# Layer 0's MLP in two stages over both halves, with seven-product groups, and a denser selection in blocks 2 to 7

## Chip, core and metric

The kernel runs on one core of a Trainium2 chip. The metric is device time of one execution in microseconds (us), from the start of the program to its end; several executions are timed and the median is given. A profile of one further execution shows each engine: PE (TensorE, the matrix engine; PEld is its weight load), DVE (VectorE), ACT (ScalarE), POOL (GpSimd) and SP (SyncE, which here only issues DMAs). Each engine works through its own instructions in program order and waits on semaphores for the others.

## What is computed

Two decoder layers on a sequence of 1024 tokens of width 1024, in float32. Layer 0 mixes tokens by attention over selected keys (mixer A), layer 1 by a sliding window (mixer B); both read a fixed memory and end in a gated MLP with a causal convolution of width 3.

```python
for i in range(DEPTH):                                  # DEPTH = 2
    h = rmsnorm(x, g_mix[i])
    mix, q_mem = mixer_a(h, ...) if i == 0 else mixer_b(h, ...)
    mem_o = memory_cross_attention(q_mem, mem_n, w_mem_kv[i])
    x = x + jnp.concatenate([mix, mem_o], axis=-1) @ w_out
    x = x + conv_glu_ffn(rmsnorm(x, g_ffn[i]), f_w_up[i], f_conv_w[i], f_conv_b[i], f_w_down[i])
return rmsnorm(x, g_final)

# in mixer_a, for each block of 128 queries (8 blocks): only the 256 best-scored keys are read
score = jnp.where(causal[None], score, -jnp.inf)
_, idx = lax.top_k(score, 256)

def conv_glu_ffn(h, w_up, conv_w, conv_b, w_down):      # D_FF = 2816
    a, b = jnp.split(h @ w_up, 2, axis=-1)
    a = sum(conv_w[j] * a_pad[:, j:j + S] for j in range(3)) + conv_b
    return (jax.nn.silu(a) * b) @ w_down
```

## The kernel before, in words

**Tiles.** Activations lie feature-major: a tile `t` holds 128 features by 2 x 512 tokens. Tokens come in two halves of 512, features of the MLP in NF = 22 tiles of 128 (tile f has a column of `a` and a column of `b`). Every float32 product is made of three matmuls (`mm3`, L256 to L258) of a rounded high part and a low rest; a weight of 128 x 1024 is loaded by SP, its high part made by ACT (L99) and its rest by POOL in two pieces (`rest`, L279). `Weights` loads five ahead and splits `SPLIT` = 2 ahead. All SBUF work tiles share 51 slots. PSUM has four tiles `pB` (128 x 512) and two tiles `pS` (128 x 1024).

**Order.** Nothing is scheduled by a planner: the Python code emits the instructions in their order. Work that is to lie beside the matmuls is a generator; `tick(ns)` moves a clock along with the matmuls emitted and advances each generator by the time it yields. So a yield's size says how densely a background work is spread, and `finish_bg` emits what is left of one at once. Stores go to SP 4 us of that clock later than they are asked for.

**Selection.** `topk` (L1230 to L1321) finds for a set of blocks the 256th best score by 32 rounds of a bit search: in each, DVE counts for one part of the blocks (L1254), ACT for the other (`sign`, L1274), and DVE makes the next candidates (L1265, L1267, twice). Then come passes on DVE alone that settle ties and make masks (L1286 to L1321). Blocks 2 and 3 run beside the query projections (`a_q`), with a yield of 1400 per step; the rest of it is emitted by `finish_bg` ahead of the third unit of attention of half 0. Blocks 4 to 7 run beside half 0's attention (`run_a`) and beside half 0's MLP, with a yield of 2400.

**Layer 0.** Half 0: `run_a`, output projection (`every`), the MLP (`ffn`). Then the same for half 1. `ffn` works on input with the gain but without the norm's scale (`prepare`, `gained`), so that matmuls can start before the norm is known; the scale multiplies `a` (L801, DVE) and the gated value (L811, POOL). For each tile: 24 matmuls for `a`, 24 for `b`; convolution on DVE (L803, L804), Silu on ACT (L810), the product with `b` on DVE (L816). After each second tile the down projection of an earlier pair (48 matmuls into `pS`) is added to x by DVE (L867). The gated values stay in SBUF. All weights are loaded and split once per half.

**Layer 1.** `ffn_up` works on normed input of both halves at once: three tiles in the plain way for each half, then 19 tiles by `group`, which makes the four products of two input halves by two token halves from seven products of half size (84 matmuls for both halves of a tile where the plain way takes 96). The factors on the input's side are made by `right_factors`, those of the weights by `Weights._factor`. Gated values go to DRAM (`keep`, `G_d`), and `ffn_down` reads them back (`fetch`) for both halves with one load of each weight.

## Time and profile before

| | us |
|---|---|
| median of 3 runs | 2623.87 (2623.51 to 2623.92) |
| the profiled execution | 2622.18 |
| its span, first to last instruction | 2620.4 |
| PE busy | 2457.7 (94%), 11912 instructions |
| DVE busy | 1702.1 (65%) |
| POOL busy | 1389.7 (53%) |
| ACT busy | 1205.3 (46%) |

In the profile, "busy" is the time in which an engine has an instruction in work, and a wait is given with the engine, tile and line that ended it. The trace gives these stretches: the query projections run from 209.5 to 359.1, half 0's attention and output projection from 378.6 to 530.6, half 0's MLP with what follows it to 945.9, half 1's attention and output projection to 1113.4, half 1's MLP to 1507.5, layer 1's MLP from 1904.1 to 2603.0.

### The profile page before, as it was taken

To read this page: it belongs to the slowest core of one execution; us is meant where nothing else is said; L and a number is where in the kernel's file an instruction comes from. 1 tells how busy PE (TensorE), PEld (TensorE's weight loads), DVE (VectorE), ACT (ScalarE), POOL (GpSimd) and SP (SyncE) were. 2 spreads that over 40 slices of the span, in tenths; PEclk is the share of its full clock that TensorE was granted. 3 is DMA by queue.
4 is the path that set the end of the run, shared out by engine and by line. 5 is a ranking of instruction groups with operands and counts; after the bars stand their busy time and mean duration, and the time that the engine had idled before them with its cause. 6 is when DMAs were issued, how large, how long until landed. Compare 5 with 4: busy or idle time off the path is not lost. (4 is left out here: it accounts for less than half of the span.)

```text
span 2620.4 us, 34001 instructions
## 1 busy us (share of the span) xinstructions
PE 2457.7 (94%) x11912; PEld 2057.2 (79%) x11912; DVE 1702.1 (65%) x2961; ACT 1205.3 (46%) x2268; POOL 1389.7 (53%) x1241
## 2 busy tenths in 40 slices
PE   7789977999998999999999989999989999999997
PEld 5677866877886888877888878878767888888886
DVE  7887878867777466655553353498786556564446
ACT  5355665645543555433333334588644444442003
POOL 5644133456666633365766665566656666664204
PEclk8899998999999999999999999999989999999999
DMA  5453353422223343332333345642253232348401
GB/s 202 149 168 116 119 173 127 157 79 98 97 74 99 133 161 101 113 101 82 107 122 97 99 117 187 216 139 86 81 193 137 105 121 97 124 170 330 141 15 65
DMA packets 121083, 333.83 MB, mean 127 GB/s; under 512 B 13008, under 2 KB 29904, under 8 KB 120912
## 3 DMA queue, kind: packets, MB, share of 16 engines
q1 hardware_dynamic: 120912, 331.66, 37.7%
q8 instruction: 94, 1.54, 0.2%
q14 instruction: 77, 0.63, 0.1%
HBM read 258.21 MB, written 73.40 MB: 127 GB/s over the span
## 5 line engine op out<-in xcount | busy, mean ns | idle before, releaser
L279 POOL TENSOR_TENSOR t<-t,t 128x512 fp32r<-128x512 f32 x829 | 1109.4, 1369 | 686.6 <-ACT t L99 283.3
L256 PE MATMUL pB<-t,t 128*128 128x512 f32 (+3 forms) x1824 | 682.5, 374 | 9.0 <-DVE t L781 4.1
L258 PE MATMUL pB<-t,t 128*128 128x512 f32 (+3 forms) x1824 | 679.0, 372 | 5.4 <-POOL t L279 5.4
L257 PE MATMUL pB<-t,t 128*128 128x512 f32 (+3 forms) x1824 | 679.6, 373 | 4.5 <-DVE t L461 2.4
L256 PE MATMUL pS<-t,t 128*128 128x512 f32 (+1 forms) x1460 | 573.3, 393 | 45.8 <-DVE t L867 19.4
L257 PE MATMUL pS<-t,t 128*128 128x512 f32 (+1 forms) x1460 | 567.9, 389 | 2.6 <-DVE t L512 2.6
L258 PE MATMUL pS<-t,t 128*128 128x512 f32 (+1 forms) x1460 | 567.1, 388 | 2.7 <-POOL t L279 2.4
L256 PEld LDWEIGHTS pB<-t,t 128*128 128x128 f32 (+1 forms) x1824 | 347.0, 190 | 69.1 <-DVE t L781 4.7
L258 PEld LDWEIGHTS pB<-t,t 128*128 128x128 f32 (+1 forms) x1824 | 346.6, 190 | 66.9 <-POOL t L279 6.7
L257 PEld LDWEIGHTS pB<-t,t 128*128 128x128 f32 (+1 forms) x1824 | 346.8, 190 | 64.2 <-DVE t L461 3.3
L256 PEld LDWEIGHTS pS<-t,t 128*128 128x128 f32 x1460 | 281.3, 193 | 104.6 <-ACT t L99 21.0
L99 ACT CAST t<-t 128x1024 fp32r<-128x1024 f32 x284 | 288.2, 1043 | 101.3 <-PE pS L258 44.1
L258 PEld LDWEIGHTS pS<-t,t 128*128 128x128 f32 x1460 | 280.8, 192 | 62.0 <-POOL t L279 6.3
L257 PEld LDWEIGHTS pS<-t,t 128*128 128x128 f32 x1460 | 281.6, 193 | 53.8 <-DVE t L512 3.0
L265 DVE TENSOR_TENSOR t<-pB,t 128x512 fp32r<-128x512 f32 (+3 forms) x248 | 149.8, 623 | 87.2 <-ACT t L264 84.6
L264 ACT CAST t<-pB 128x512 fp32r<-128x512 f32 (+3 forms) x248 | 126.2, 535 | 160.2 <-PE pB L258 99.7
L1055 DVE TENSOR_TENSOR t<-t,pS 128x1024 f32<-128x1024 f32 (+1 forms) x92 | 107.9, 1174 | 125.6 <-PE pS L258 125.4
L867 DVE TENSOR_TENSOR t<-t,pS 128x1024 f32<-128x1024 f32 x88 | 106.9, 1217 | 54.8 <-PE pS L258 54.5
L811 POOL TENSOR_TENSOR t<-t,t 128x512 f32<-128x512 f32 x44 | 58.4, 1328 | 155.0 <-ACT t L810 155.0
L1447 POOL TENSOR_SCALAR t<-t,st 128x128 f32<-128x128 f32 (+3 forms) x64 | 47.8, 749 | 138.3 <-DVE st L1446 77.8
L1274 ACT ACTIVATE sign<-t,ti 128x1024 bf16<-128x1024 f32 (+1 forms) x96 | 96.5, 1006 | 52.5 <-DVE ti L1267 39.6
L1222 DVE SCALAR_TENSOR_TENSOR t<-t,wtok,t 128x384 f32<-128x384 f32 (+5 forms) x90 | 98.8, 1098 | 22.6 <-ACT t L1217 18.7
(228 smaller groups left out, 3018.9 us busy)
## 6 DMA issues: line engine op xcount, KB each, us to landing
t<-in_up SPq DMA_DIRECT2D x138, 512.0 KB
t<-in_down SPq DMA_DIRECT2D x66, 512.0 KB
G_d<-t SPq DMA_DIRECT2D x44, 512.0 KB
t<-G_d SPq DMA_DIRECT2D x44, 512.0 KB
t<-in_a_in SPq DMA_DIRECT2D x34, 512.0 KB
t<-in_b_in SPq DMA_DIRECT2D x28, 512.0 KB
t<-in_a_out SPq DMA_DIRECT2D x20, 512.0 KB
t<-x_d SPq DMA_DIRECT2D x20, 512.0 KB
```

The source lines that it names most:

```text
L99: nc.scalar.copy(hi[:, :w], raw[:, :w])
L256: mm(out, a[0], b[0], start=start, stop=False, skip_group_check=again)
L257: mm(out, a[0], b[1], start=False, stop=False, skip_group_check=again)
L258: mm(out, a[1], b[0], start=False, stop=stop, skip_group_check=again)
L264: nc.scalar.copy(hi, src)
L265: nc.vector.tensor_tensor(lo, src, hi.bitcast(F32), op=OP.subtract)
L279: self.nc.gpsimd.tensor_tensor(lo[:, s], src[:, s], hi[:, s].bitcast(F32), op=OP.subtract)
L811: nc.gpsimd.tensor_tensor(v, v, rb[0], op=OP.mult)
L867: nc.vector.tensor_tensor(x[dp][:, :, t], x[dp][:, :, t], S, op=OP.add)
L1055: nc.vector.tensor_tensor(xp, xp, S, op=OP.add)
L1222: nc.vector.scalar_tensor_tensor(work[:, :n], tmp[:, :n], wv, work[:, :n], op0=OP.mult, op1=OP.add)
L1274: nc.scalar.activation(hits("sign")[:, :wide], self.work[blks[i]][:, :wide], AF.Sign, bias=cand[:, i:i + 1].bitcast(F32), accum_out=cnt[:, ...
```

## The change

- Layer 0's MLP is made as layer 1's: an up stage that writes the gated values to DRAM, then `ffn_down` for both halves. The up stage of half 0 takes its first four tiles on unscaled input and goes on with normed input until the selection and the first two units of half 1's attention are emitted; the program that results has 17 tiles there. Half 1 takes the same 17 tiles in the same way, and the last five tiles go through `ffn_groups` (formerly the second part of `ffn_up`).
- `right_factors` for layer 0 also rebuilds half 0's split input from DRAM (`h0`). The scale is applied once (`finish`), and the mult on POOL (L811) stays for the first four tiles alone.
- Weights are split four ahead in these stages. `conv` reads `a` from PSUM where the input is normed.
- Selection: blocks 2 and 3 with a yield of 1000 instead of 1400; blocks 4 to 7 with 1200 instead of 2400 from the MLP on.
- The memory units of half 1 begin after the selection, so most of their second parts now lie in half 1's attention. The keys and values of layer 1's memory and the norm of half 0 lie in `ffn_down`.

```diff
-    def ffn(self, l, halves, fold=1, last=None, then=None):
...
+    def ffn_half(self, l, fs, hf, h, rb=None, ahead=None):
+        nc, name = self.nc, f"up{l}"
+        for f in fs:
+            a, b = self.psB(), self.psB()
+            wa = self.w.get(name, f)
+            first = rb is not None and not rb
...
+            self.proj(a, wa, h)
...
+            if rb:
+                nc.vector.tensor_tensor(v, a, rb[0], op=OP.mult)
+            self.conv(l, f, hf, v if rb else a, u)
+            if not first:
+                wb = self.w.get(name, NF + f)
...
+                self.proj(b, wb, h)
+            nc.scalar.activation(u, u, AF.Silu)
+            if rb:
+                nc.gpsimd.tensor_tensor(u, u, rb[0], op=OP.mult)
+            nc.vector.tensor_tensor(u, u, b, op=OP.mult)
+            self.keep(f, hf, u)
...
-            bt.append(self.add_bg(self.topk((2, 3), 1400, (3,))))
+            bt.append(self.add_bg(self.topk((2, 3), [1000], (3,))))
...
-            late.append(self.add_bg(self.topk((4, 5, 6, 7), 2400, (6, 7))))
+            late.append(self.add_bg(self.topk((4, 5, 6, 7), late_pace, (6, 7))))
...
+        def finish(x, sqs, rb, gain, h, wait, keep, dst):
+            yield from self.scale_of(sqs, rb, wait)
+            del sqs[:]
+            yield from self.norm_apply(rb[0], x, gain, 2, h, 2500, keep=keep)
+            yield from self.store_x(x, dst)
...
+        last = self.run_a(0, att, x, mem_o, bm, hook)
+        late[1] = 0.0
+        self.every(last)
...
+        late[1], late_pace[0] = 1.0, 1200
...
+        self.w.SPLIT = self.AHEAD
+        self.ffn_half(0, range(4), 0, raw, rb)
+        del raw[:]
+        while len(h0) < 4:
+            self.tick(100)
+        n_half = 4
+        while bt in self.bg:
+            self.ffn_half(0, [n_half], 0, h0)
+            n_half += 1
...
+        last = self.run_a(1, att, x, mem_o, bm, hook)
+        self.every(last)
...
+        bT = self.add_bg(self.right_factors(hf1, h1, B, h0))
+        self.w.SPLIT = self.AHEAD
+        self.ffn_half(0, range(4), 1, raw, rb)
...
+        self.ffn_half(0, range(4, n_half), 1, h1, ahead=self.AHEAD)
+        self.finish_bg(bn, bT)
...
+        self.ffn_groups(0, b11, b21, b22, B, range(n_half, NF), self.near_down(xs))
...
+        bk = self.add_bg(mem_kv(), 0.4)
...
+        self.ffn_down(0, xs, [hook0, hook1], 3)
+        self.finish_bg(bk)
```

How the order moves is seen at three places. `t` are work tiles, `ti`, `tc` and `hit` the selection's candidates, counts and marks.

DVE, at the end of the query projections, from the memory queries' evacuation (L620, L622) on; first before, then now (the count, L1254, is L1213 there):

```order
L715 TENSOR_REDUCE st<-pB 128x2
L620 SCALAR_TENSOR_TENSOR t_3573<-pS,t_3573 64x1024
L622 SCALAR_TENSOR_TENSOR t_3574<-pS,t_3574 64x1024
L1265 TENSOR_SCALAR ti<-tc 128x1
L1267 SCALAR_TENSOR_TENSOR ti<-ti 128x1
L1254 TENSOR_SCALAR hit,tc<-t_1134,ti 128x384
```

```order
L715 TENSOR_REDUCE st<-pB 128x2
L620 SCALAR_TENSOR_TENSOR t_3638<-pS,t_3638 64x1024
L622 SCALAR_TENSOR_TENSOR t_3639<-pS,t_3639 64x1024
L265 TENSOR_TENSOR t_3658<-pB,t_3658 128x384
L1398 ISA t_3665,st<-pB,t_1134 128x384
```

Before, the rest of the selection of blocks 2 and 3 (45 DVE and 4 ACT operations in the source) stands between L622 and the next evacuation of a `pB` (L265); now none of it does, and it all stands earlier.

DVE, at the start of half 0's MLP, the sum of squares that the norm's matmul (PE, L424) waits for; before, then now:

```order
L412 TENSOR_TENSOR t_5119<-t_5119,t_5143 128x1024
L412 TENSOR_TENSOR t_5119<-t_5119,t_5174 128x1024
L404 TENSOR_TENSOR t_5119<-t_5119 128x512
L404 TENSOR_TENSOR t_5198<-t_5198 128x512
L412 TENSOR_TENSOR t_5119<-t_5119,t_5198 128x512
```

```order
L412 TENSOR_TENSOR t_5119<-t_5119,t_5143 128x1024
L1213 TENSOR_SCALAR hit,tc<-t_1921,ti 128x640
L412 TENSOR_TENSOR t_5119<-t_5119,t_5174 128x1024
L1213 TENSOR_SCALAR hit,tc<-t_2241,ti 128x768
L1224 TENSOR_SCALAR ti<-tc 128x2
L1226 SCALAR_TENSOR_TENSOR ti<-ti 128x2
L404 TENSOR_TENSOR t_5119<-t_5119 128x512
L404 TENSOR_TENSOR t_5198<-t_5198 128x512
L412 TENSOR_TENSOR t_5119<-t_5119,t_5198 128x512
```

Now operations of the selection stand between the sums; before, the selection started again only behind the norm.

ACT, one tile of half 0's MLP in the middle of the bit search, from one convolution's start to the next; before, then now (L1233 is L1274 before, L862 is L802, L908 is L810, L875 is L820):

```order
L802 ACTIVATE t_6234<-t_6234,conv 128x512
L806 COPY prev_a<-t_6234 128x2
L810 ACTIVATE t_6234<-t_6234 128x512
L820 CAST t_6272<-t_6234 128x512
L99 CAST t_6278<-t_6110 128x1024
L1274 ACTIVATE sign,tc<-t_2525,ti 128x1024
L1274 ACTIVATE sign,tc<-t_2846,ti 128x1024
L99 CAST t_6320<-t_6187 128x1024
L802 ACTIVATE t_6325<-t_6325,conv 128x512
```

```order
L862 ACTIVATE t_6041<-pB,conv 128x512
L866 COPY prev_a<-pB 128x2
L99 CAST t_6048<-t_5997 128x1024
L1233 ACTIVATE sign,tc<-t_2567,ti 128x1024
L1233 ACTIVATE sign,tc<-t_2902,ti 128x1024
L908 ACTIVATE t_6041<-t_6041 128x512
L875 CAST t_6091<-t_6041 128x512
L99 CAST t_6098<-t_6046 128x896
L1233 ACTIVATE sign,tc<-t_2567,ti 128x1024
L1233 ACTIVATE sign,tc<-t_2902,ti 128x1024
L862 ACTIVATE t_6142<-pB,conv 128x512
```

A tile now carries two rounds of the search where it carried one.

## Rows read from the trace of the kernel before

**Rows 1.** The page, parts 1 and 2: PE's busy time, its granted clock in slices.

```profile
PE 2457.7 (94%) x11912; PEld 2057.2 (79%) x11912; DVE 1702.1 (65%) x2961; ACT 1205.3 (46%) x2268; POOL 1389.7 (53%) x1241
...
PEclk8899998999999999999999999999989999999999
```

**Rows 2.** Stretches: length, busy us (instructions) of PE, PEld, DVE, ACT, POOL; clock, DMA.

```profile
209.50:359.00 149.50, 144.10 (x673) 119.28 (x672) 120.70 (x231) 97.34 (x209) 36.64 (x31) 0.99 0.31 100
...
432.00:520.00 88.00, 88.00 (x524) 76.67 (x523) 76.18 (x201) 60.46 (x132) 39.10 (x45) 1.00 0.50 168
...
753.50:822.30 68.80, 59.46 (x254) 48.40 (x252) 64.49 (x74) 15.85 (x22) 41.87 (x25) 0.95 0.31 99
...
1904.00:1991.00 87.00, 74.69 (x301) 58.46 (x300) 69.19 (x75) 40.27 (x51) 50.24 (x32) 0.92 0.53 188
1991.00:2353.00 362.00, 362.00 (x1599) 299.75 (x1598) 210.62 (x317) 158.91 (x286) 227.85 (x175) 1.00 0.34 118
```

**Rows 3.** PE and DVE in order of time, 378 to 404: start, us, line, wait.

```profile
378.81 1.47 PE L1434 MATMUL pB<-t,t 128*128 128x384 f32 x6
403.78 0.58 PE L713 MATMUL pB<-t,t 128*128 128x256 f32 x1 [23.50 <-DVE t L265]
...
382.53 1.23 DVE L622 SCALAR_TENSOR_TENSOR t<-pS,t 64x1024 fp32r<-64x1024 f32 x1
...
403.16 0.56 DVE L265 TENSOR_TENSOR t<-pB,t 128x384 fp32r<-128x384 f32 x1
```

**Rows 4.** DVE's waits, 200 to 380: for whom, us in total, times, longest.

```profile
DVE t L1222 <- ACT t L1217: 18.7, 26, 1.4
```

**Rows 5.** PE's waits in half 0's MLP, 530.6 to 946.

```profile
PE pS L256 <- DVE t L867: 14.3, 5, 7.9
PE pS L424 <- DVE t L412: 4.9, 1, 4.9
```

**Rows 6.** PE and DVE in order of time around the first norm of half 0's MLP.

```profile
543.77 1.87 PE L424 MATMUL pS<-ones,t 128*128 128x1 f32 x8 [4.88 <-DVE t L412]
...
542.08 1.63 DVE L412 TENSOR_TENSOR t<-t,t 128x512 f32<-128x512 f32 x1
```

**Rows 7.** DVE by line, 556 to 823: count, busy us, mean ns, idle before.

```profile
L1254 DVE TENSOR_SCALAR_CACHE_REDUCE hit<-t,ti 128x768 bf16<-128x768 f32 x21 | 21.2, 1008 | 0.3
L1267 DVE SCALAR_TENSOR_TENSOR ti<-ti 128x2 int32<-128x2 int32 x42 | 20.3, 482 | 1.4
L1254 DVE TENSOR_SCALAR_CACHE_REDUCE hit<-t,ti 128x640 bf16<-128x640 f32 x21 | 18.3, 873 | 0.0
L1265 DVE TENSOR_SCALAR ti<-tc 128x2 int32<-128x2 f32 x42 | 16.9, 403 | 0.7 <-ACT sign L1274 0.2
```

**Rows 8.** Two such small operations in order of time, DVE, from 739.

```profile
739.81 1.22 DVE L1265 TENSOR_SCALAR ti<-tc 128x2 int32<-128x2 f32 x1
741.06 0.16 DVE L1267 SCALAR_TENSOR_TENSOR ti<-ti 128x2 int32<-128x2 int32 x1
```

**Rows 9.** DVE by line in layer 1's plain tiles, 1935 to 1992.

```profile
L944 DVE SCALAR_TENSOR_TENSOR t<-pB,conv,t 128x511 f32<-128x511 f32 x5 | 3.7, 742 | 3.5 <-ACT t L943 3.5
L971 DVE TENSOR_TENSOR t<-t,pB 128x512 f32<-128x512 f32 x5 | 3.4, 683 | 2.7 <-PE pB L258 1.4 <-ACT t L970 1.3
```

**Rows 10.** PE's waits in half 0's attention, 378.6 to 530.6.

```profile
PE pB L752 <- DVE t L265: 1.6, 4, 0.8
```

**Rows 11.** PE's waits in half 1's MLP, 1113.4 to 1507.5.

```profile
PE pS L256 <- DVE t L867: 5.1, 5, 2.4
PE pS L424 <- DVE t L412: 3.9, 1, 3.9
PE pB L443 <- DVE st L439: 2.8, 1, 2.8
```

**Rows 12.** PE's waits in layer 1's plain tiles, 1904 to 1991, and in its down stage.

```profile
PE pB L258 <- POOL t L279: 5.4, 3, 3.3
...
PE pS L256 <- DVE t L1012: 1.8, 1, 1.8
```

More of the change, by code (lines that the diff above doesn't have):

```diff
@@ new lines, in keep @@
+    def keep(self, f, hf, u):
+        t = self.t4(2, HT, dt=R32)
+        self.nc.scalar.copy(t[:, 0], u)
+        self.rest(t[:, 1], u, t[:, 0])
+        self.store("G", self.G_d[f][hf], t.bitcast(F32))
+    def ffn_half(self, l, fs, hf, h, rb=None, ahead=None):
+        nc, name = self.nc, f"up{l}"
+        for f in fs:
+            a, b = self.psB(), self.psB()
+            wa = self.w.get(name, f)
+            first = rb is not None and not rb
+            if first:
+                split = self.w.SPLIT
+                self.w.SPLIT = max(3, split)
+                wb = self.w.get(name, NF + f)
+            self.proj(a, wa, h)
+            uv = self.t4(2, HT)
+            u, v = uv[:, 0], uv[:, 1]
+            if first:
+                self.proj(b, wb, h)
+                while not rb:
+                    self.tick(100)
+                self.w.SPLIT = split
+            if rb:
[3 more added lines that the diff above has]
+                wb = self.w.get(name, NF + f)
+                if ahead and f == fs[-1]:
+                    self.w.SPLIT = ahead
+                self.proj(b, wb, h)
+            nc.scalar.activation(u, u, AF.Silu)
[3 more added lines that the diff above has]
+            self.keep(f, hf, u)
+            del a, b, uv, u, v, wa, wb
@@ L1015, in group @@
             yield
-            keep(f, 0, ua)
+            self.keep(f, 0, ua)
             tt(ub, ub, c22, op=OP.mult)
             yield
-            keep(f, 1, ub)
+            self.keep(f, 1, ub)
         before = iter(())
-        for f in range(n_std, NF):
+        for f in fs:
             g = group(f)
@@ L1060, in weights @@
             return [self.w.get(f"down{l}", 2 * c + i) for i in range(2)]
-        for c in range(nch - 2):
+        for c in range(nch - tail):
             us = weights(c)
             for hf in range(2):
-                if c + 1 + hf < nch:
-                    fetch(c + 1, hf)
+                self.fetch(c + 1, hf)
                 down(c, us, G.pop((c, hf)), hf)
-        us = [weights(c) for c in (nch - 2, nch - 1)]
-        for hf in range(2):
-            fetch(nch - 1, hf)
-        for hf in range(2):
-            for c, u in zip((nch - 2, nch - 1), us):
-                down(c, u, G.pop((c, hf)), hf)
+        us, cs = {}, range(nch - tail, nch)
+        order = [(c, hf) for hf in range(2) for c in cs]
+        for i, (c, hf) in enumerate(order):
+            if hf == 0:
+                us[c] = weights(c)
+            for e in order[i + 1:i + 3]:
+                if e not in G:
+                    self.fetch(*e)
+            down(c, us[c], G.pop((c, hf)), hf)
     def a_small(self, hf, h):
@@ L1493, in begin_a @@
             yield s()
+        while not selected():
+            yield 500
         for u in units[:2]:
@@ L1720, in run @@
         self.exps = []
-        self.cn, self.work, self.vB, self.qm, self.marks = {}, {}, {}, {}, set()
+        self.cn, self.work, self.vB, self.qm, self.marks, self.G = {}, {}, {}, {}, set(), {}
         self.scratch()
@@ new lines, in run, with memory, begin @@
+        h0, rb = [], []
+        bn = self.add_bg(finish(x, sqs, rb, g[:, 3], h0, 1000, lambda i, t: self.store("hf", self.hf_d[i], t),
+                                self.x_d[0]))
+        del x
+        late[1], late_pace[0] = 1.0, 1200
+        mem = self.mem_units(1)
+        def memory():
+            while late in self.bg:
+                yield 1000
+            self.load_qmem(1)
+            yield 9000
+            yield from self.whole(mem[0], 2200)
+        att = self.attn_a(1)
+        def begin():
+            while ("found", 4) not in self.marks:
+                yield 500
+            yield from self.spread(self.begin_a(att, lambda: late not in self.bg), 2950)
```

357 lines of the change are left out of this document (138 added, 219 removed).

## The prediction

> **What bounds the kernel now.** I read the page first: PE is busy for 94% of the span, at full clock nearly everywhere [rows 1]. So time goes away only where PE gets fewer matmuls, or where one of its waits ends. The stretches come next. In layer 1's groups PE never waits: 1599 matmuls in 362.0 us, 0.2264 us each [rows 2]. That is the pace; a stage's **loss** is its length minus its large matmuls at that pace, minus some 0.15 us for each small one (an estimate, by width). A loss is a wait and the slower clock behind it. Last I read PE's waits by stage, and who ended them.
>
> - Half 0's attention: one wait of 23.5 us. PE stands from 380.3 to 403.78 for a `pB` that DVE empties at 403.16; DVE had been ready at 383.8 (382.53 + 1.23) and then worked through the rest of the selection of blocks 2 and 3 [rows 3].
> - Half 0's MLP (415 us): 1584 large matmuls at the pace are 358.6, some 164 small ones 24, so 33 are lost; the two largest waits are 14.3 for the additions into x, on two `pS`, and 4.9 for the first norm [rows 5].
> - Half 1's MLP (394 us): 358.6, and 116 small ones for 16, so 20 are lost; waits 5.1, 3.9 and 2.8 [rows 11].
>
> **Part 1: five tiles by seven products.** A tile takes 84 matmuls instead of 96 for both halves, 5 x 12 = 60 fewer, 60 x 0.2264 = **-13.6 us**. The groups' additions on DVE and splits on POOL are those of layer 1, where DVE is busy for 58% and POOL for 63% and PE does not wait [rows 2]. Without that cover the five groups (95 us) would lose what layer 1's plain tiles lose (below), 23% or 22 us. The down stage has as many matmuls as before and needs each weight once instead of twice; its transfers through DRAM lie beside it, as in layer 1, where it waits once, 1.8 us [rows 12].
>
> **Part 2: blocks 2 and 3 sooner.** What stands between 383.8 and 403.2 on DVE is emitted earlier, so PE's `pB` comes at about 384.9: 18.9 us are saved, and some 4.6 stay, in which DVE empties the memory queries. The 19 us of DVE work now lie in the query projections, where DVE was busy for 120.7 of 149.5 us [rows 2]: it comes to some 139, 93%. The cover is DVE's own idle time: 18.7 us in 26 holes of 0.7 us, behind ACT [rows 4]. The highest share that a stage without a wait of PE shows is 76.18 of 88.0, 87% [rows 2]. So the added loss lies between 0 and the 9 us by which 139 exceeds 87% of 149.5; I take 4. **-15 us** (bounds -19 and -10).
>
> **Part 3: half 0's up stage.** It has 17 tiles, 816 large matmuls, 185 us, for a selection that had 350. Two losses are to be expected.
>
> *The first norm.* The sum that PE's L424 waits for is ready at 543.7, when PE has waited 4.9 us [rows 6]. Now two counts and three pairs of small operations, or four, stand among the sums: about 0.87 + 1.01 + 0.87 and six times 0.44 [rows 7], 5 us more. The wait is 10 us; with the slow clock behind it, as now, the first tile loses 14 instead of 7.
>
> *VectorE's balance.* A round of the search costs DVE 1.01 + 0.87 + 2 x (0.48 + 0.40) + 0.16 = 3.8 us [rows 7]. From the first tile to the search's end there are 438 matmuls, 99 us, and 18 rounds, 68; nine convolutions and products at 2 x 0.74 + 0.68 [rows 9], 19; the norm's multiplications and rests, 11 (an estimate at 1.0 and 1.2 us); the scaling of `a` in four tiles, 3. That is 101. The passes behind the search were 46 us of DVE: 64.5 busy [rows 2] less eight additions and three tiles' convolution, 18. Now they fall into 47 us of matmuls, with four tiles' work and evacuations, 11: 57. Together 158 us of work in 146. DVE can't be busy all the time, since it waits for ACT's `sign`; in the passes it reached 94%, in the attention 87%. At 92% the 158 take 172, and DVE falls 26 us behind. PE notices only when it needs a `pB` back: there are four, two per tile, so one is needed again three projections (3 x 24 x 0.2264 = 16.3 us) after it is full, less 2.3 for the convolution: 14 us of backlog are free, and weights split four ahead leave about as much. So 12 us are lost here, and after the passes 44 us of matmuls with 17 us of DVE work clear the rest. At 100% the loss is 0, at 85% it is 26. Loss of the stage: 14 + 12 = 26 instead of 33, **-7 us** (bounds -19 and +7). ACT comes close too: four `sign` a tile.
>
> A row speaks against this sum. The small operations of a round take 0.16 us, or 1.22, in the same stretch [rows 8], and in the mean 0.40 and 0.48 [rows 7]. The Trainium skill (SBUF — State Buffer, "Who interferes with whom") says that a DVE instruction with two SBUF inputs, or in a two-port mode, and a GpSimd instruction that reads SBUF exclude each other for the whole instruction. By that, the convolution from PSUM (0.74, with one input in SBUF) should be spared, which the trace agrees with, and a denser search may be blocked more often; the sum above takes the mean as it was.
>
> **Part 4: half 1's attention.** It waits for nothing now. 36 matmuls of the memory units' second parts are left to be emitted at once there, as 48 were in half 0's, where they cost several short waits, four of up to 0.8 us for one cause [rows 10], and slow clock, some 5 us in all. **+4 us** (0 to +8).
>
> **Part 5: half 1's MLP and the down stage.** The additions' waits go with `ffn`'s interleaving [rows 11]; the first norm's stays (7 us with the slow clock). Layer 1's start, with norm and factors beside plain tiles, loses 20 of 87 us, waiting for splits [rows 2, 12]; four splits ahead instead of two should cover all but some 2. The down stage adds its start, 1.8 us, with slow clock 3, and the norms of the memory and of half 0, now on its two `pS`, 8: one such wait is 2.8 [rows 11], twice, with slow clock. 20 against 20: **0 us** (-6 to +8). Layer 1's own code is the same but for names and the order of temporaries; nothing is counted.
>
> **Sum.** -13.6 - 15 - 7 + 4 + 0 = -31.6. The profiled execution took 2622.18, so 2590.6; the median of the runs is 1.7 above it: **2592 us**.
>
> **Rivals.**
>
> *VectorE's backlog is free* (chance 0.17). It keeps at 95% or more; half 0 loses the first norm alone, and the query projections nothing: 2592 - 12 - 4 = 2576. For it: no `pB` of the MLP made PE wait before, however late DVE was. Against: the balance above.
>
> *The selection's denser part gains nothing* (0.12). The query projections turn DVE-bound: the added 19 us reappear as waits for evacuation. 2592 + 15 = 2607. For it: 93%. Against: the holes.
>
> *The splits starve* (0.09). ACT stands behind DVE in both halves, and the splits come late as in layer 1's plain tiles; 23% on half 1's tiles 4 to 12, nine of 10.9 us, is 23 us: 2615.
>
> *VectorE and GpSimd lock each other out; slower* (0.10). If every small operation of the 18 rounds took 1.22 instead of 0.44 us [rows 7, 8], 72 x 0.78 = 56 us come on top of a backlog that is past what is free: 2592 + 56 = 2648. It decides in half 0's MLP, and the kernel is slower than before from 32 us on, when more than half are blocked. For it: POOL's splits are as dense as before while the search is twice as dense. Against: a third were blocked before. The skill's rule above is this rival's; blocked each time is its upper end.
>
> *The change does what it says*: 17 and 5 tiles are in the order, so no chance is set aside for the contrary.
>
> **How the numbers follow.** The forecast has 0.52, the others 0.17, 0.12, 0.09 and 0.10. The forecast's own bounds: all good ends -13.6 - 19 - 19 + 0 - 6 = -58, all bad ones -13.6 - 10 + 7 + 8 + 8 = -1; taken as independent about half of that on either side, 2576 to 2608. The range takes in the first two rivals with their spread and most of the third, 2568 to 2616; outside are the locked case, and the edges, 2 in 10. Within 0.2% (5 us, about what a measurement of this kernel can tell from no change) is 2619 to 2629: 0.06, from the bad ends of the second and third. Slower: 0.11, the lock and a little. Faster: 0.83.
>
> **What would show it.** Right: 60 fewer matmuls; PE's wait for L713 at about 5 us instead of 23.5; a wait for L424 near 10 us; in half 0's tiles waits of PE for a `pB` or a split in the passes behind the search, 5 to 20 us; none for additions into x in half 0's stretch. Wrong: a DVE that is idle in half 0's tiles while PE waits (then it is ACT, POOL or SP that I have costed at nothing); waits on L279 or L99 in half 1's tiles or groups; a loss of over 10 us in the query projections; a clock below full in the down stage. What would make it wrong most easily is the share that DVE can keep up, which no stage of before shows at this density.

## The result, and the profile after

The changed kernel takes 2664.82 us, median of 4 runs (2661.78 to 2666.09); the kernel before took 2623.89. The ratio is 1.0153, with a 95% interval of 1.0138 to 1.0169: **slower** by 41 us, 1.5%. The prediction was 2592, its range ended at 2616. The profiled execution took 2664.9, its span is 2663.1.

The page shows the 60 matmuls gone (11852 where [rows 1] has 11912), PE busy for 13.6 us more all the same, and a lower clock in half 0's MLP and in half 1's.

```profile
PE 2471.3 (93%) x11852; PEld 2060.0 (77%) x11852; DVE 1751.2 (66%) x3005; ACT 1204.9 (45%) x2284; POOL 1295.2 (49%) x1164
...
PEclk9799999989999998999999999999999999999999
```

To say where the time went I took the prediction's loss for every stage: its length minus what its matmuls take at the median distance that their shape keeps in the same trace. The two spans differ by 42.7 us, and this is how they come about (the last column is what the prediction's terms make of the loss before; "rest" is the difference of all other stages together):

| stage | loss before | loss after | difference | predicted loss |
|---|---|---|---|---|
| query projections and the step behind them | 12.0 | 22.1 | +10.1 | 16 |
| half 0's attention | 34.5 | 14.2 | -20.3 | 15.6 |
| half 0's MLP | 33.0 | 47.9 | +14.9 | 26 |
| half 1's attention | 1.8 | 17.1 | +15.3 | 5.8 |
| half 1's MLP and down stage | 19.6 | 45.2 | +25.6 | 20 |
| layer 1's plain tiles | 19.9 | 27.1 | +7.2 | 19.9 |
| rest | | | +3.3 | 0 |
| matmuls | | | -13.4 | -13.6 |

The terms fall short by some 74 us together: 25 in half 1's MLP and down stage, 22 in half 0's MLP, 11 in half 1's attention, 7 in layer 1's plain tiles, and 8 in the rest.

The stretches of after, columns as in [rows 2]: query projections; what follows up to the end of half 0's attention; half 0's four unscaled tiles; its other 13; half 1's attention; its four unscaled tiles; its other 13; the five groups; the down stage; layer 1's plain tiles.

```profile
210.70:367.60 156.90, 148.15 (x673) 121.83 (x672) 128.75 (x275) 99.23 (x216) 34.09 (x27) 0.97 0.29 94
367.60:521.90 154.30, 143.62 (x830) 123.23 (x829) 128.19 (x318) 104.94 (x228) 65.47 (x80) 0.98 0.52 177
521.90:585.40 63.50, 50.45 (x206) 41.03 (x205) 50.04 (x88) 33.04 (x49) 33.68 (x23) 0.87 0.28 96
585.40:769.60 184.20, 164.88 (x710) 132.88 (x709) 147.71 (x242) 106.85 (x179) 110.55 (x85) 0.95 0.43 149
769.60:949.80 180.20, 173.39 (x1085) 153.69 (x1084) 112.67 (x220) 93.38 (x191) 62.86 (x65) 0.96 0.38 125
960.70:1021.00 60.30, 49.04 (x205) 39.17 (x203) 46.36 (x50) 22.09 (x27) 35.80 (x23) 0.94 0.22 71
1021.00:1181.60 160.60, 148.02 (x624) 121.11 (x625) 83.45 (x93) 64.04 (x82) 93.04 (x70) 0.95 0.44 154
1181.60:1276.80 95.20, 95.20 (x421) 78.83 (x421) 52.24 (x78) 42.00 (x73) 59.27 (x46) 1.00 0.37 129
1276.80:1541.10 264.30, 255.50 (x1172) 211.00 (x1172) 143.49 (x158) 45.11 (x55) 78.72 (x61) 1.00 0.46 169
1939.80:2033.50 93.70, 77.36 (x301) 59.42 (x300) 73.22 (x75) 40.87 (x51) 49.82 (x32) 0.91 0.51 182
```

The groups run at the full pace, as predicted: PE is busy for all of their 95.2 us. The loss stands in the plain tiles on either side. PE's waits there, for half 0's tiles (521.9 to 769.6; engine, for whom, us in total, times, longest), where [rows 5] has additions and the first norm:

```profile
PE pB L256 <- DVE t L911: 11.9, 4, 6.4
PE pB L256 <- ACT prev_a L866: 8.9, 4, 3.8
PE pS L424 <- DVE t L412: 6.7, 1, 6.7
PE pB L713 <- DMA t<-qm_d: 4.7, 2, 4.4
```

and for half 1's (960.7 to 1181.6), where [rows 11] has 5.1, 3.9 and 2.8:

```profile
PE pB L256 <- DVE t L911: 13.6, 3, 5.8
PE pS L424 <- DVE t L412: 3.9, 1, 3.9
PE pB L256 <- DVE t L901: 2.7, 1, 2.7
PE pB L256 <- DVE t L864: 1.7, 1, 1.7
```

The waits for additions into x are gone from these stretches, as predicted (in the down stage, where the additions now lie, five come to 5.7 us). In their place PE waits for its own tiles' banks: L911 is VectorE's last operation of a tile (the gate times `b`), which frees a `pB`. Why it is late in half 1, where no search runs, VectorE by line shows, 1000 to 1066 (count, busy us, mean ns, idle before):

```profile
L804 DVE TENSOR_TENSOR t<-t,t 128x1024 fp32r<-128x1024 f32 x12 | 18.0, 1534 | 2.6 <-ACT t L799 2.6
L869 DVE SCALAR_TENSOR_TENSOR t<-prev_a,conv,t 128x2 f32<-128x2 f32 x4 | 4.8, 1212 | 0.1
L868 DVE SCALAR_TENSOR_TENSOR t<-prev_a,conv,t 128x1 f32<-128x1 f32 x4 | 4.6, 1158 | 0.0
...
L838 DVE TENSOR_TENSOR t<-t,t 128x1024 f32<-128x1024 f32 x2 | 3.5, 1758 | 0.0
L816 DVE TENSOR_TENSOR t<-t,t 128x1024 f32<-128x1024 f32 x2 | 3.5, 1756 | 0.0
L821 DVE TENSOR_TENSOR t<-t,t 128x1024 f32<-128x1024 f32 x2 | 3.4, 1709 | 0.0
L825 DVE TENSOR_TENSOR t<-t,t 128x1024 f32<-128x1024 f32 x2 | 3.4, 1698 | 0.1
L911 DVE TENSOR_TENSOR t<-t,pB 128x512 f32<-128x512 f32 x4 | 2.7, 682 | 5.0 <-POOL t L910 5.0
```

L804, L816, L821, L825 and L838 are `right_factors`, which the prediction didn't cost in layer 0: 20 operations, 18.0 + 3.5 + 3.5 + 3.4 + 3.4 = 31.8 us, beside three plain tiles. In order of time, VectorE and then PE:

```profile
1025.70 5.72 DVE L804 TENSOR_TENSOR t<-t,t 128x1024 fp32r<-128x1024 f32 x4
1031.35 1.21 DVE L838 TENSOR_TENSOR t<-t,t 128x1024 f32<-128x1024 f32 x1
1032.49 0.68 DVE L911 TENSOR_TENSOR t<-t,pB 128x512 f32<-128x512 f32 x1
```

```profile
1027.96 0.39 PE L258 MATMUL pB<-t,t 128*128 128x512 f32 x1
1033.31 0.77 PE L256 MATMUL pB<-t,t 128*128 128x512 f32 x1 [4.96 <-DVE t L911]
...
1033.30:1039.00 5.70, 5.69 (x14) 4.44 (x15) 3.25 (x2) 2.41 (x3) 4.74 (x3) 0.50 0.54 166
```

PE stands for 4.96 us while VectorE works off five factor operations in front of the one that frees the bank, and then goes on, for twelve matmuls and until 1039, at 0.43 us each instead of 0.2264. The last line is this stretch, with columns as in [rows 2]: the granted clock is 0.50 in it, the lower of the two levels. This is the slow clock behind a wait.

### The profile page after: what moved, and what is told of

It reads as the page before. It is cut to its first block, busy times and chain, and to the rows that moved or that the text cites. A ratio compares the mean times of both kernels' runs of the same rounds, so it can differ in the third digit from the quotient of the medians.

```text
span 2663.1 us, 34000 instructions
## 1 busy us (share of the span) xinstructions
PE 2471.3 (93%) x11852; PEld 2060.0 (77%) x11852; DVE 1751.2 (66%) x3005; ACT 1204.9 (45%) x2284; POOL 1295.2 (49%) x1164
## 5 line engine op out<-in xcount | busy, mean ns | idle before, releaser
L279 POOL TENSOR_TENSOR t<-t,t 128x512 fp32r<-128x512 f32 x788 | 1061.6, 1375 | 960.8 <-ACT t L99 404.8
L256 PE MATMUL pB<-t,t 128*128 128x512 f32 (+2 forms) x1744 | 661.6, 379 | 56.6 <-DVE t L911 26.9
L258 PE MATMUL pB<-t,t 128*128 128x512 f32 (+2 forms) x1744 | 655.7, 376 | 5.7 <-POOL t L279 5.7
L257 PE MATMUL pB<-t,t 128*128 128x512 f32 (+2 forms) x1744 | 656.6, 376 | 4.7 <-DVE t L461 2.4
L256 PE MATMUL pS<-t,t 128*128 128x512 f32 (+1 forms) x1520 | 594.8, 391 | 34.5 <-ACT t L99 19.4
L257 PE MATMUL pS<-t,t 128*128 128x512 f32 (+1 forms) x1520 | 590.5, 389 | 1.9 <-DVE t L512 1.9
L258 PE MATMUL pS<-t,t 128*128 128x512 f32 (+1 forms) x1520 | 590.5, 388 | 1.7 <-POOL t L279 1.4
L256 PEld LDWEIGHTS pB<-t,t 128*128 128x128 f32 (+1 forms) x1744 | 337.5, 194 | 122.4 <-issue 28.5
L258 PEld LDWEIGHTS pB<-t,t 128*128 128x128 f32 (+1 forms) x1744 | 336.9, 193 | 67.0 <-POOL t L279 8.0
L257 PEld LDWEIGHTS pB<-t,t 128*128 128x128 f32 (+1 forms) x1744 | 337.3, 193 | 62.0 <-DVE t L461 3.3
L256 PEld LDWEIGHTS pS<-t,t 128*128 128x128 f32 x1520 | 292.7, 193 | 94.8 <-ACT t L99 22.9
L1012 DVE TENSOR_TENSOR t<-t,pS 128x1024 f32<-128x1024 f32 (+1 forms) x180 | 215.0, 1196 | 218.9 <-PE pS L258 218.7
L258 PEld LDWEIGHTS pS<-t,t 128*128 128x128 f32 x1520 | 291.7, 192 | 61.7 <-POOL t L279 4.4
L257 PEld LDWEIGHTS pS<-t,t 128*128 128x128 f32 x1520 | 292.2, 192 | 55.7 <-DVE t L512 2.4
L99 ACT CAST t<-t 128x1024 fp32r<-128x1024 f32 (+1 forms) x242 | 248.6, 1045 | 113.7 <-PE pS L258 44.5
L265 DVE TENSOR_TENSOR t<-pB,t 128x512 fp32r<-128x512 f32 (+3 forms) x248 | 149.5, 623 | 77.1 <-ACT t L264 74.6
L863 DVE SCALAR_TENSOR_TENSOR t<-pB,conv,t 128x511 f32<-128x511 f32 x56 | 41.9, 749 | 139.9 <-ACT t L862 138.1
L105 ACT CAST t<-t 128x512 fp32r<-128x512 f32 x168 | 101.2, 617 | 60.7 <-DVE t L122 33.6
L1233 ACT ACTIVATE sign<-t,ti 128x1024 bf16<-128x1024 f32 (+1 forms) x96 | 96.8, 1009 | 65.3 <-DVE ti L1226 52.7
L1181 DVE SCALAR_TENSOR_TENSOR t<-t,wtok,t 128x384 f32<-128x384 f32 (+5 forms) x90 | 96.3, 1070 | 20.8 <-ACT t L1176 16.9
```

The source lines that it names most:

```text
L99: nc.scalar.copy(hi[:, :w], raw[:, :w])
L105: nc.scalar.copy(hl[:, 0], src)
L256: mm(out, a[0], b[0], start=start, stop=False, skip_group_check=again)
L257: mm(out, a[0], b[1], start=False, stop=False, skip_group_check=again)
L258: mm(out, a[1], b[0], start=False, stop=stop, skip_group_check=again)
L265: nc.vector.tensor_tensor(lo, src, hi.bitcast(F32), op=OP.subtract)
```

## Experiments

The runs came in groups, each on one chip with the kernel before beside it (2621.8 to 2623.6, by group). "After" is 2664.8.

**e1: the copy of two columns first.** In `conv`, line 866 moved up:

```
         nc.scalar.activation(u, a, AF.Identity, ...)
+        if hf == 0:
+            nc.scalar.copy(prev, a[:, HT - 2:])
         nc.vector.scalar_tensor_tensor(u[:, 1:], ...)
```

> One edit to the changed kernel: in half 0 ScalarE copies the two last columns of a (prev_a, L866) ahead of VectorE's two convolution steps instead of behind them. Theory A (the added time is PE waiting for banks and splits that hang on handoffs between in-order engines): in the changed kernel PE waits 8.9 us in half 0's plain tiles for this copy by itself, and ScalarE waits 31.9 us for VectorE there with weight casts queued behind it; with the slow clock behind each wait about 12 to 18 us go, 2648 to 2653. Layer 1's plain tiles of half 0 have the same copy, 1 to 3 us more. Rival B (VectorE's sheer load is the bound in half 0, and whoever waits for the copy would wait for VectorE anyhow): under 4 us, 2661 or more.

Measured: 2656.37, 8.4 less. But half 0's MLP loses 49.0, against 47.9: nothing was gained where the wait was. PE's waits there now read (L866 is VectorE's second convolution step in this kernel):

```profile
PE pB L256 <- DVE t L866: 12.1, 6, 3.3
PE pB L256 <- DVE t L911: 8.8, 3, 6.4
```

The 8.9 us for ScalarE's copy have become 12.1 for VectorE. The copy was only the last link; VectorE is late. Rival B holds for half 0, though the time fell by more than it allowed. The gain lies elsewhere: 6.9 in half 1's attention (a stage that by itself lost 11.8, 14.9 and 14.5 in e2 to e4, where nothing in it was edited, so that part of the 6.9 is spread) and 2.6 in layer 1's plain tiles.

**e2: the right factors 4500 apart.**

```
-    def right_factors(self, hf1, h1, out, h0=None):
+    def right_factors(self, hf1, h1, out, h0=None, pace=1400):
...
-            yield 1400
+            yield pace
...
-        bT = self.add_bg(self.right_factors(hf1, h1, B, h0))
+        bT = self.add_bg(self.right_factors(hf1, h1, B, h0, 4500))
```

> One edit to the changed kernel: the steps of the right factors in layer 0's half 1 come 4500 planner ns apart instead of 1400, so that VectorE's 20 subtractions and small rests lie over tiles 5 to 15 instead of 4 to 6. Theory A (half 1 lost 25.6 us against before because these subtractions, which the prediction costed at nothing, stand on VectorE beside the first plain tiles): the waits of PE from 1012 to 1062 (18 us with those of the last unscaled tile) shrink to a third, 10 to 16 us less, 2649 to 2655. Rival B (the unscaled tiles' own chain and the first norm are what is lost there): within 4 us of the changed kernel, 2661 to 2667.

Measured: 2643.97, 20.8 less. The 13 tiles' stretch and PE's only wait in it:

```profile
1014.60:1157.50 142.90, 141.97 (x626) 116.93 (x624) 84.68 (x93) 62.68 (x81) 92.95 (x69) 1.00 0.51 176
```

```profile
PE pB L256 <- DVE t L911: 0.9, 1, 0.9
```

VectorE has the same work in it (84.7 us, before the edit 83.5), but spread over it, and the loss falls from 18.9 to 1.3. So the factors' place was worth 17.6 us; the rest is what half 1's attention (5.3 less) and the down stage (6.2 more) vary by. Theory A, and somewhat more than it said.

**e3: the five tiles as plain ones.** The groups are replaced by ten plain tiles, and the factors by a routine that reads half 0's input back and splits it:

```
-        bT = self.add_bg(self.right_factors(hf1, h1, B, h0))
+        bT = self.add_bg(self.reload(h0))
...
-        self.ffn_groups(0, b11, b21, b22, B, range(n_half, NF), self.near_down(xs))
...
+        self.ffn_half(0, range(n_half, NF), 0, h0)
...
+        self.ffn_half(0, range(n_half, NF - 2), 1, h1)
+        near(NF - 2)
+        self.ffn_half(0, range(NF - 2, NF), 1, h1)
```

> The changed kernel with its five Strassen tiles of layer 0 as plain tiles of both halves (60 matmuls more), and without the right factors: half 0's input is only read back and split. If the groups are worth their 60 matmuls and the factors' subtractions cost nothing, it is 13.6 us slower than the changed kernel, 2678. Theory A (the factors cost half 1 about 15 us beside its first plain tiles): 13.6 lost and 10 to 18 gained, 2660 to 2668. Rival B (plain tiles without a search beside them lose 23% as layer 1's did): ten tiles of 10.9 us lose 20 us more, about 2690.

Measured: 2656.15, 8.7 less than with the groups, although PE has 60 matmuls more. Half 1's 13 scaled tiles and the ten plain ones, which have neither search nor factors beside them, lose nothing, 1018.9 to 1269.2:

```profile
1018.90:1160.40 141.50, 141.50 (x626) 117.18 (x626) 62.55 (x73) 55.11 (x71) 93.27 (x73) 1.00 0.48 167
1160.40:1269.20 108.80, 108.80 (x482) 90.12 (x481) 29.98 (x40) 39.63 (x55) 63.19 (x50) 1.00 0.45 155
```

Rival B, the plain tiles' own 23%, is out. Against e2 it is 2656.15 - 2643.97 = 12.2 us slower: that is what the groups are worth when their factors are out of the way, close to the 13.6 of the count. As the change packs them, the factors cost more than the groups save.

**e4: blocks 2 and 3 at 1400 again.**

```
-            bt.append(self.add_bg(self.topk((2, 3), [1000], (3,))))
+            bt.append(self.add_bg(self.topk((2, 3), [1400], (3,))))
```

> One edit to the changed kernel: the selection of blocks 2 and 3 has its step of 1400 again instead of 1000. Theory A (by the two traces: half 0's attention lost 20.3 us less, the query projections and the step behind them 10 us more): 10 us slower, 2671 to 2677. Rival B (the wait saved at the attention's start comes back elsewhere, nothing is gained): within 3 us, 2662 to 2668. Rival C (the prediction's term): 15 us slower, 2680.

Measured: 2672.52, 7.7 more. The losses of the query projections and of the step behind them go back to 11.7, half 0's attention to 35.0. By the stages the part is worth 10, by the runs 8: theory A, of its size the lower end.

**e5: half 0's MLP without the search.** The 18 rounds behind half 0's attention are left out, so that this kernel's selection of blocks 4 to 7 is a coarse one; the tiles stay as they were. In `topk`, and so for the counts and steps:

```
+                run = nb < 4 or pace[0] != 1200
-                if len(own) + k < nb:
+                if len(own) + k < nb and run:
                     ...sign...
```

> The changed kernel without the instructions of the search's rounds in half 0's MLP (the 18 rounds of blocks 4 to 7 behind half 0's attention, counts, signs and steps, are left out; their places in the order stay empty, so that the number of tiles and everything else stands as it was; the selection of those blocks is then a coarse one). Theory A (the 47.9 us that half 0's MLP loses are mostly the search on VectorE and ScalarE among 17 tiles): the waits from 578 to 645 go, about 15 us with the slow clock behind them, and the first norm gets 2 to 4 us shorter: 2643 to 2650. Rival B (the unscaled tiles' own chain over GpSimd and the first norm are what is lost): under 6 us, 2659 or more.

Measured: 2633.48, 31.3 less, more than theory A said. Half 0's MLP loses 19.2 instead of 47.9:

```profile
520.40:577.40 57.00, 48.06 (x205) 39.10 (x204) 39.55 (x48) 20.99 (x28) 36.29 (x24) 0.94 0.28 98
577.40:739.20 161.80, 157.58 (x710) 129.84 (x710) 93.81 (x121) 73.22 (x120) 111.63 (x87) 0.99 0.51 175
```

The search's 18 rounds cost 28.7 us, of which 22.4 in the 13 scaled tiles. 12.2 of the four unscaled ones' 18.4 are not the search's.

**e6: the search at 1600.** On top of e2:

```
-        late[1], late_pace[0] = 1.0, 1200
+        late[1], late_pace[0] = 1.0, 1600
```

> The kernel of e2_factors_spread with a second edit: the search in half 0's MLP has a step of 1600 instead of 1200; half 0's stage then has 20 tiles instead of 17, and two tiles instead of five are left for the groups. Theory A (density is what costs in half 0): the groups that go cost 3 x 12 x 0.2264 = 8.2 us, the stage's loss of 48 falls by 10 to 18: 2634 to 2642 against 2644. Rival B (the search costs the same whatever its step): 2650 to 2654.

Measured: 2633.05, 10.9 less than e2. Half 0's stage, now 20 tiles, loses 34.9 instead of 48.5; three groups fewer cost 8.2 us of matmuls; the down stage and half 1's attention lost 7 less, which is no more than they vary by in runs that leave them alone. PE's largest wait in the stage:

```profile
PE pB L256 <- DVE ti L1224: 7.0, 2, 5.8
```

Density is what costs (theory A), and a wider step than the changed kernel's pays for the groups that it takes away.

**e7: memory units earlier, layer 1's factors earlier.** On top of e2:

```
-            yield 9000
-            yield from self.whole(mem[0], 2200)
+            yield 5000
+            yield from self.whole(mem[0], 1400)
...
-            while len(h1) < 3 + j:
+            while len(h1 if h0 is not None else hf1) < 3 + j:
```

> The kernel of e2_factors_spread with two edits in two other stages: the memory units of half 1 come 1400 apart instead of 2200, and start 4000 earlier, so that no second part is left for half 1's attention; and layer 1's right factors start, as in the kernel before, when the normalised input is there, not its split. Theory A (36 second parts at once and the late start are what half 1's attention loses, 17.1 against 1.8; the later start of the factors is what layer 1's plain tiles lose, 27.1 against 19.9): 8 to 14 and 4 to 7 less, 2624 to 2632. Rival B (the units only take their loss with them into half 0's tiles, where VectorE and ScalarE are late too; layer 1's loss is from another order of the temporaries): 2640 to 2646.

Measured: 2644.50, nothing gained. Half 1's attention loses 6.1 instead of 11.8, but half 0's MLP 56.8 instead of 48.5, where PE now waits longest for the load of the memory queries:

```profile
PE pB L713 <- DMA t<-qm_d: 9.3, 2, 8.9
```

Layer 1's tiles lose 25.9 instead of 27.1. Rival B for both: the second parts took their loss with them, and layer 1's earlier start was worth 1.2.

**e8: the kernel before with 1000 for blocks 2 and 3.** In the old kernel:

```
-            bt.append(self.add_bg(self.topk((2, 3), 1400, (3,))))
+            bt.append(self.add_bg(self.topk((2, 3), 1000, (3,))))
```

> The kernel before with one edit: the step of the selection of blocks 2 and 3 is 1000 instead of 1400. Theory A (this part does in the kernel before what it does in the changed one, where undoing it cost 7.7 us): 2613 to 2617. The prediction's term of 15 us: 2608. Rival B (half 0's MLP of before takes the gain back, as VectorE comes earlier to the search of blocks 4 to 7): 2621 to 2625.

Measured: 2613.57, 8.6 less than before; ratio 0.9964, interval 0.9953 to 0.9976. It is the fastest kernel of this study. The wait of [rows 3] is as long as in the changed kernel, and VectorE's share of the query projections too (columns as in [rows 2]):

```profile
397.25 0.38 PE L713 MATMUL pB<-t,t 128*128 128x256 f32 x1 [3.22 <-DVE t L265]
```

```profile
212.10:368.80 156.70, 147.75 (x674) 121.75 (x673) 128.81 (x275) 99.14 (x216) 34.12 (x27) 0.97 0.29 95
```

So this part of the change does the same thing in both kernels. Theory A, and the prediction's 15 us are out.

**e9: layer 1's factors by the old routine; unscaled tiles split two ahead.** On top of e6:

```
-        bT = self.add_bg(self.right_factors(hf1, h1, B))
+        bT = self.add_bg(self.right_factors1(hf1, B))     # the routine of the kernel before
...
-        self.w.SPLIT = self.AHEAD
         self.ffn_half(0, range(4), 0, raw, rb)
+        self.w.SPLIT = self.AHEAD
```

(and so for half 1).

> The kernel of e6_search_1600 with two edits in different stages. Layer 1's right factors are formed by the routine of the kernel before (same operations, its order, no temporary overwritten); and layer 0's four unscaled tiles of either half split their weights two ahead as before, four ahead only from the fifth tile on. For layer 1's plain tiles: theory A (the routine's order costs the 7 us) 27.4 falls to about 20; rival B (other temporaries and weights held longer) stays at 26 to 28. For the unscaled tiles: theory A (early splits on GpSimd stand in front of its product with rb, for which VectorE and then PE wait) the losses of 17.4 and 14.0 fall by 3 to 6 each; rival B (sums and search ahead of the first norm, whatever the splits) they stay within 2, or rise as PE waits for splits. Both A: 2633 less 13 to 19, 2614 to 2620; both B: 2631 to 2636.

Measured: 2632.93, as e6, from parts that cancel. Layer 1's plain tiles lose 20.6 instead of 27.4: theory A. The old routine orders its operations otherwise and overwrites no operand, and this run can't tell the two apart. The unscaled tiles lose 22.4 and 19.7 instead of 17.4 and 14.0: rival B, early splits help them. In half 0 that only moves the loss, for its other 16 tiles lose 11.5 instead of 17.6; in half 1 it is a loss of 5, and the down stage, where nothing was edited, loses 3 more.

**e10: the kernel before with 1200 for blocks 2 and 3.** The edit of e8, with 1200.

> The kernel before with a step of 1200 for the selection of blocks 2 and 3, half way between 1400 and e8_before_p23_1000. Theory A (the wait at the attention's start is what is left of the selection and shrinks with the step, the cost in the query projections grows with density): wait 10 to 14 us, loss in the projections and the step behind them 15 to 18 against 12 and 23, time 2616 to 2620. Rival B (the projections' loss comes only from the last bit of density): 2610 to 2614.

Measured: 2619.47; ratio 0.9992, 0.9982 to 1.0001. The wait is 16.3 us, longer than theory A's 10 to 14, and the loss in the projections and behind them 17.3. Half the step takes the whole cost's half (5.3 of 10) but a third of the wait (7.2 of 20.3); theory A's time, and no gain that is clear of no change.

**e11: the repairs together.** e6, with layer 1's old routine and the copy of e1.

> The repairs that helped, together: the kernel of e6_search_1600 with layer 1's factors by the old routine and with the copy of prev_a ahead of VectorE's convolution. If the effects of the single runs add up (layer 1: 6.8 us; the copy: 3 to 8): 2618 to 2624, which is the kernel before within its own spread, and still above e8_before_p23_1000. If the copy's gain was spread of the stages around half 1's attention and not the copy's: 2624 to 2628.

Measured: 2619.02; ratio 0.9985, 0.9975 to 0.9995. Layer 1's plain tiles lose 17.0, half 1's attention 8.8, half 0's MLP 31.3. The repairs add up, and make of the changed kernel one that is 0.15% faster than before, and 5 us slower than e8, where one number was changed.

**e12: half 0's MLP without ScalarE's signs.** VectorE's counts and steps stay and work on old sums for blocks 6 and 7.

```
-                if len(own) + k < nb:
+                if len(own) + k < nb and (nb < 4 or pace[0] != 1200):
                     ...sign...
```

> The changed kernel without ScalarE's share of the search in half 0's MLP (the sign instructions of the 18 rounds for blocks 6 and 7 are left out; VectorE's counts and steps stay, with old sums for those two blocks; the selection of the two is then wrong). e5_no_search took 28.7 us off the loss of 47.9. Theory A (VectorE's load and its place in the order is the bound): half 0's stage loses 40 or more, 2656 to 2666. Rival B (ScalarE's two signs a round stand in front of the convolution, the SiLU and the weight casts, and VectorE waits behind them): the loss falls by 15 or more, 2640 to 2650.

Measured: 2654.36, 10.4 less. Half 0's stage loses 39.5 instead of 47.9. The signs cost 8.4 of the search's 28.7 us, which leaves 20.3 for VectorE's counts and steps with what waits for them. Neither theory's number for the loss is met (40 or more; 15 less), and the time lies between their ranges; A is the nearer.

**e13: six unscaled tiles, the norm's steps 4500 apart.** On top of e11 (and so for half 1):

```
-            yield from self.norm_apply(rb[0], x, gain, 2, h, 2500, keep=keep)
+            yield from self.norm_apply(rb[0], x, gain, 2, h, 4500, keep=keep)
...
-        self.ffn_half(0, range(4), 0, raw, rb)
+        self.ffn_half(0, range(6), 0, raw, rb)
```

> The kernel of e11_repairs with one more edit: six tiles instead of four on unscaled input in either half of layer 0, and the steps that apply the norm (VectorE, ScalarE and GpSimd) 4500 apart instead of 2500. Theory A (the unscaled tiles lose 17 and 14 us, against 7.7 and 7.6 of before, because the norm's multiplications and rests, which the kernel before didn't have, stand among them): with the steps over six tiles the stage starts lose 3 to 6 less each: 2608 to 2614. Rival B (the first norm's own wait and the slow clock behind it are the loss; the two more tiles cost VectorE a multiplication each): within 3 us of 2619, or up to 5 more.

Measured: 2619.37, as e11. Half 0's MLP loses 30.3 (31.3), half 1's plain tiles 16.1 (15.3). In half 1, spreading the norm moves the loss to later tiles: the six unscaled ones lose 11.3 where four lost 14.1, the others 4.8 instead of 1.2. Rival B by its number; what the unscaled tiles lose beyond the first norm and the search, some 5 to 8 us in each half (12.2 in e5 and 15.4 against 7.7 and 7.6 for the same matmuls before), stays open.

## Why the prediction was wrong

Three steps of it failed: it left the factors' operations out of layer 0 (parts 1 and 5), it took VectorE's share at this density as 92% and put the loss in the wrong place (part 3), and it counted nothing for layer 1 (part 5). Parts 2 and 4 had the right mechanism and too kind a size.

**Part 1 (five tiles, -13.6): right in the matmuls, wrong in what comes with them.** The count is right (-13.4 by the trace, 12.2 between e2 and e3), and so is the groups' pace. The failing step is "The groups' additions on DVE and splits on POOL are those of layer 1": it priced the groups and left out `right_factors`, which feeds them. In layer 1 its 16 operations were part of a stretch that loses 20 us, a loss that was in the table [rows 2, 12] and that the prediction put down to splits. In layer 0 it is 20 operations, 31.8 us of VectorE, in a stage that had none, and cost 17.6 (e2). The missing term alone turns the -13.6 into a loss of 4.

**Part 2 (-15): right in the mechanism, a third to a half too large.** PE's wait went from 23.5 to 3.2, a little better than the 4.6 predicted. But the query projections and the step behind them lose 10.1 more, not 4, and more than the bound of 9. Of the 19 us of VectorE's work only 8 came to lie in the projections (128.75 us where [rows 2] has 120.70); the stretch got 7.4 us longer, so that VectorE is busy for 82% of it and not 93%. It could not use the holes of [rows 4], which are handoffs from ScalarE: they are nearly as large as before, and PE's wait behind them has doubled. The first line is of before, 209.5 to 404; the others are of after, 210.7 to 395 (L1173, L1176 and L1181 are L1214, L1217 and L1222 of before).

```profile
PE pB L1214 <- ACT t L1217: 3.9, 3, 2.4
```

```profile
PE pB L1173 <- ACT t L1176: 8.8, 6, 2.8
```

```profile
DVE t L1181 <- ACT t L1176: 16.9, 22, 1.5
```

Runs give 7.7 (e4) and 8.6 (e8).

**Part 3 (loss 26, -7): the load was right; the share was not, nor where the loss falls, and the size is off by 22.** It is 47.9. The wait for the first norm was 6.7, less than the 10 predicted. The work in the balance held: up to the search's end VectorE has 104.8 us of it (101 predicted), in the passes behind the search 62.0 (57), columns as in [rows 2]:

```profile
538.70:673.10 134.40, 116.07 (x473) 92.57 (x472) 104.77 (x208) 86.10 (x136) 68.57 (x53) 0.93 0.38 133
673.10:736.20 63.10, 57.80 (x257) 47.70 (x258) 62.00 (x72) 20.23 (x32) 39.50 (x24) 0.94 0.52 188
```

The failing step is "At 92% the 158 take 172", with a backlog that PE notices in the passes. VectorE is busy for 78% of the first stretch, in which PE loses 27.9, and for 98% of the second, in which it loses 8.4. So it is not work piled up that PE waits for: VectorE stood idle beside a waiting PE, the prediction's own sign of being wrong. By the prediction's own scale (26 lost in the tiles behind the first at 85%, and 14 for the first norm) a share below 85% means 40 and more. Where VectorE's idle time goes is in its rows, 521.9 to 645 (the last columns are its idle time and whom it waited for):

```profile
L1226 DVE SCALAR_TENSOR_TENSOR ti<-ti 128x2 int32<-128x2 int32 x32 | 18.4, 574 | 1.1
...
L1224 DVE TENSOR_SCALAR ti<-tc 128x2 int32<-128x2 f32 x32 | 11.2, 351 | 3.0 <-ACT sign L1233 2.5
...
L911 DVE TENSOR_TENSOR t<-t,pB 128x512 f32<-128x512 f32 x7 | 4.8, 687 | 12.6 <-POOL t L910 9.4 <-ACT t L908 3.1
...
L863 DVE SCALAR_TENSOR_TENSOR t<-t,conv 128x511 f32<-128x511 f32 x4 | 3.0, 751 | 3.7 <-ACT t L862 3.7
...
L863 DVE SCALAR_TENSOR_TENSOR t<-pB,conv,t 128x511 f32<-128x511 f32 x3 | 2.2, 749 | 5.0 <-ACT t L862 5.0
```

It is idle for 28 us of these 123, and 21.3 of them are spent at the head of its queue on a step of the *tile* (the product with rb on GpSimd, ScalarE's SiLU and first convolution step), with the search's work behind it in the order. The prediction expected the waits at `sign`; they are 2.5 us. That the search costs 28.7 is shown (e5), and that a wider step makes it cheaper (e6). That it does so by these handoffs, each of which holds an in-order queue, is read from the rows: no run took a handoff of VectorE's own away, and e1 moved only ScalarE's copy, without any gain there.

**Part 4 (+4): too small.** The attention of half 1 lost 15.3 more in the profiled run, and 10 to 13 more in e2 to e4. The step counted the 36 second parts; behind it came also a late VectorE (1.4 us for L911 of the last tile) and the units' first parts. e7 moved the second parts out, and the stage lost 6.1; but half 0's tiles lost 8 more. In the one earlier place that was tried it costs as much.

**Part 5 (20 against 20): wrong, mostly by the term missing from part 1.** 45.2: 18.9 in the 13 tiles (the factors), 15.4 in the unscaled ones and 11.0 in the down stage (the 11 predicted). For the 13 tiles the prediction had layer 1's start before it, "with norm and factors beside plain tiles", put its loss down to splits, and said that four splits ahead "should cover all but some 2"; PE waited for no split here, and 18.9 were lost, 17.6 of them to the factors (e2). The unscaled tiles were put at 7, as before; the norm's application, which the kernel before did not have, stands among them, and one wait of 2.8 for L911 comes right behind it. That it is the cause is not shown, for e13, which spreads the norm, gains nothing. "Layer 1's own code is the same but for names and the order of temporaries; nothing is counted" is the third failing step: the rewritten factor routine cost 7 us (e9). It starts later, has another order and overwrites its operands; the start alone was worth 1.2 (e7).

**The rivals.** "VectorE and GpSimd lock each other out", the slower case, gave 2648 and is the nearest, but not by its mechanism: the two small operations of a round take 574 + 351 = 925 ns in the mean, and took 885 in [rows 7]; the search was hardly blocked more often. Where the lock does show is in the factors: an operation that takes 1.21 us takes 2.20 in layer 1. "The splits starve" named the right stretch of half 1, but PE waited for banks there, not for splits. A new stream of VectorE work beside plain tiles, the largest single term that was missing (17.6 of some 74 us), was not among them.

## What to carry to other kernels

When a faster product is moved to a new place, cost the preparation of its operands there operation by operation, and look at which tiles it will stand beside: here 32 us on an engine that was 52% busy over the stage cost 18, and next to nothing when spread. An engine's busy share at its density of today says little of what it can keep up when two chains share its in-order queue: here 92% was assumed, and it kept 78 to 82% where both chains went back and forth between engines, and 98% in the passes, which run on it alone. Count the handoffs of each. A one-number edit inside a large change (here the step of one selection) deserves a run by itself; as the change stood, it was the only part shown to pay.

## What the runs showed of the hardware

- The same subtraction over 128x1024 elements takes VectorE 1.21 us (L816, L838) or 2.20 (L821, L825) in one stretch of layer 1, with GpSimd busy for half of it. The four of 2.20 begin while GpSimd is at work on a rest (L279), the four of 1.21 while it is not. 1978 to 2034:

```profile
L821 DVE TENSOR_TENSOR t<-t,t 128x1024 f32<-128x1024 f32 x2 | 4.4, 2200 | 0.1
...
L816 DVE TENSOR_TENSOR t<-t,t 128x1024 f32<-128x1024 f32 x2 | 2.4, 1215 | 0.0
```

  Operations on 128x1 and 128x2 elements (L868, L869) take 0.21 us beside an idle GpSimd, or 1.2. In half 1's first tiles 8 of these cost 9.4 us together, more than the convolution's large steps. The Trainium skill (SBUF — State Buffer, "Who interferes with whom") says that a VectorE instruction with two inputs in SBUF and a GpSimd instruction that reads SBUF exclude each other; these rows agree with it.
- The slow clock behind PE's waits added a quarter to a half of them: half 1's 13 tiles lost 18.9 us with 15.2 of waits, half 0's 29.4 with 19.3. Granted clocks of 0.95 in either stretch, and 1.00 where no wait is, are the same thing read from the rows.
- The stores of the up stage's results stand on SP's queue until GpSimd has made the rest, and loads queue behind them. SP waited 104.6 us so between 645 and 770:

```profile
SPq L202 <- POOL t L279: 104.6, 11, 16.8
```

  PE's 4.7 us for the memory queries (`qm_d`) end with a load in that queue, issued at 728.29, just behind a store that had waited 16.8 us. A run with the stores on another queue was not made, so what the queue costs is not shown.
